# A diffusion step on one core: the last step of an adaLN quarter moves from VectorE to products in the bank, with a written order for two stages

## The chip, the cores and the metric

The kernel runs on one core of a Trainium2 chip. The metric is the device time of one execution in microseconds. An execution of the kernel before was also recorded by the hardware profiler; the rows quoted below come from that record. Engine names: PE is TensorE's matmuls, PEld its weight loads, DVE is VectorE, ACT is ScalarE, POOL is GpSimd, SP is SyncE, which issues nearly all DMA transfers.

## The reference, cut to what matters

One step of a two-layer network with d = 2048 over two groups of 128 tokens: a context pass and a denoising step. Both use the same weights. Every layer does this, once per group:

```python
mod = silu(cond) @ w_ada[l] + b_ada[l]              # 2048 -> 6 * 2048
sh1, sc1, gt1, sh2, sc2, gt2 = split(mod, 6)
h = rmsnorm(x, g_norm_mix[l]) * (1 + sc1) + sh1
m = mixer(h)                                        # layer 0: A + B, layer 1: C
x = x + gt1 * m
h = rmsnorm(x, g_norm_ffn[l]) * (1 + sc2) + sh2
x = x + gt2 * conv_ffn(h)                           # 2048 -> 2 * 5632 -> conv -> 2048
```

Mixer A + B (latent attention and grouped attention) has one input projection `w_in_ab` and one output projection `w_out_ab`; mixer C (differential attention) has `w_in_c` and `w_out_c`. A final RMSNorm and the six new cache tensors end it. All is float32. `cond` has one row per group, so `mod` has two columns for each of its 12288 elements, while its weights `w_ada` are 2 x 2048 x 12288 floats.

## The kernel before, in words

**Layout.** Activations lie transposed: features on the 128 partitions in 16 chunks, and 256 columns, the first 128 tokens of one group and the next 128 of the other. Every weight tile of 128 x 128 is split into a rounded high part `wh` (a copy by ScalarE, L244) and a low part `wl` (a subtraction by VectorE, L245); activations are split likewise. A tile costs three products of 256 columns (`gemm`, L104 through a helper, so all plain products have line 104; transposes have line 107). SyncE loads weights in tiles `raw` of up to 1 MB, from three buffers.

**Units.** A *unit* is a quarter (4 chunks, 512 elements) of one of the adaLN vectors of one layer, and streams 4 MB of `w_ada`. There are three ways to compute one.

- A unit of the list `ROWS` normally goes over TensorE. `row_step` loads four tiles `araw` (or `raw`) and `sum_rows` adds each into the one PSUM bank `ada`: the condition vector is the stationary side (128 x 32, two columns used), and the partial sums of four partition groups land in rows 32g and 32g+1 of the bank.
- A *side* unit (those listed in `BESIDE`, 3 in the first layer and 6 in the second) is summed by VectorE: `side_step` loads one `block` of 256 KB and `sum_block` adds it, scaled, into `aacc` (L481, two instructions a block, 16 blocks a unit). `reduce` then sums over partitions with four groups of products into the bank `misc`.
- Others go by a VectorE reduction over rows (`feature_step`, L452). They do not change.

The first two ways end in `ada_finish`, as a list of calls that are made one at each pump: `copy` (ScalarE copies the bank to `am` in SBUF, L408), then `turn`. The old `turn` transposes `am` in four blocks of 128 (two for a side unit) into a bank; VectorE then adds the partial sums with a reduce (L424; wide units) and adds the bias from the constants (L426, or L420 for a side unit) into `mod`, and for a scale vector forms the product with the norm's weights (`scales`). In the very first quarter, `half_unit` does half a unit at a time, in the same way; it is not changed.

**Stages.** The projection `w_in_ab` is done in parts over the input chunks, since the adaLN quarters come one after the other: two halves of the first quarter (h0 and h1), then quarters 1, 2, 3. Each `part` runs 23 output chunks; after a chunk it adds the result to the running sum (or copies it, the first time) and calls `pump`. Before a part `modulate` turns the normed x into the split `hx` for that quarter (VectorE `nt`, L596 and L602, ScalarE `hx`, L606), and `ensure` first finishes the two units (shift and scale) which that needs. After that come the heads of the first mixer, `w_out_ab`, norm, ConvFFN, then layer 1 in the same way.

**What sets the order.** The framework's scheduler orders the instructions of each engine by data and by its estimates, except where `keep_order` pins an instruction behind the pinned one before it. With `pe.in_turn` every TensorE instruction is pinned; before the change that is so in mixer C alone. `pump` spreads the units over the stages: it calls `side_pump` and `row_step` by rates per chunk (`RATE`, `SIDE`). `side_pump` adds the stage's `SIDE` rate to a due count and does one `side_step` per whole number; `side["apart"]` makes reduce, copy and turn wait one chunk each. `pinned[0]` pins the sums of rows from quarter 3 on, and puts each tile's sums some steps behind its load. `ada` has one buffer, `misc` one, `am` one, `block` three, and `raw` three.

## Time and profile before

| | us |
|---|---|
| median of 3 runs | 2364.11 (2363.92 to 2364.25) |
| the profiled execution | 2362.85 |
| its span | 2361.1 |
| PE busy | 2306.7 |
| DVE busy | 1847.8 |
| ACT busy | 1164.5 |
| POOL busy | 175.7 |

The span is the time from the first to the last record of the profiled execution; 1.75 us of its time lie around it. Busy times count matmuls, weight loads, vector and scalar operations, not the instructions that only issue transfers. In a timeline row the first number is the start in us from the span's start, the second the length, then engine, line, operation, output, inputs, and sizes; a bracket at the end gives how long the engine had been idle before it and what released it. In a row of groups, a count with x is followed by durations in ns.

The stages by start, in us: first part of `w_in_ab` 27.8 to 53.7, second half to 85.5, quarter 1 to 130.4, quarter 2 to 174.7, quarter 3 to 214.2, heads to about 331, output projection to 455.2, norm and first ConvFFN to 1188, layer 1 with mixer C to 1540, its output projection to 1613.6, the norm and second ConvFFN to about 2347.

### The profile page before, as it was taken

The page shows a single profiled execution, that of the slowest core. Times are in us where ns is not written, and L with a number is a line of the kernel's source. Part 1 is how long each engine was busy: PE and PEld are TensorE (multiplying, and loading weights), DVE is VectorE, ACT ScalarE, POOL GpSimd, SP SyncE. Part 2 cuts the span into 40 slices and gives each one's busy share as a digit, 9 for nine tenths or more (in the row PEclk, how much of TensorE's full clock was granted, in tenths as well). Part 3 has the DMA queues.
Part 4 walks back from the last instruction along what each step waited for, and adds up shares of the span by engine and source line. Part 5 has one row for each costly group of instructions (what it writes and reads, how often), then busy time and mean ns, then how long its engine had stood idle before and what let it go on. Part 6 is the DMA issues. An engine that isn't in the chain of part 4 may idle for free. (4 is left out here: it accounts for less than half of the span.)

```text
span 2361.1 us, 47623 instructions
## 1 busy us (share of the span) xinstructions
PE 2306.7 (98%) x19624; PEld 2183.2 (92%) x19624; DVE 1847.8 (78%) x2822; ACT 1164.5 (49%) x1857; POOL 175.7 (7%) x210
## 2 busy tenths in 40 slices
PE   6999999999999999999999999999999999999997
PEld 4778768899999999999989999998999999999997
DVE  3569866779999999999878888798899755666654
ACT  4245544465553355554464444446555534555543
POOL 0002202100000000001220000022000000000011
PEclk9999999999999999999999999999999999999999
DMA  9988888667777877777768888777677555555553
GB/s 368 360 310 283 310 316 328 248 241 251 261 265 285 303 268 260 262 259 274 285 249 279 306 295 312 249 242 271 245 260 258 198 194 197 197 195 191 192 193 124
DMA packets 108249, 612.96 MB, mean 260 GB/s; under 512 B 11712, under 2 KB 19584, under 8 KB 40832
## 3 DMA queue, kind: packets, MB, share of 16 engines
q1 hardware_dynamic: 108032, 609.92, 71.3%
q8 instruction: 154, 2.52, 0.4%
q14 instruction: 63, 0.52, 0.1%
HBM read 605.12 MB, written 4.75 MB: 258 GB/s over the span
## 5 line engine op out<-in xcount | busy, mean ns | idle before, releaser
L104 PE MATMUL acc<-hx,wh 128*128 128x256 f32 x8416 | 1456.3, 278 | 9.3 <-ACT hx L606 4.4
L104 PEld LDWEIGHTS acc<-hx,wh 128*128 128x128 f32 x8416 | 1272.6, 188 | 46.8 <-issue 16.6
L244 ACT CAST wh<-raw 128x1024 fp32r<-128x1024 f32 (+1 forms) x822 | 795.3, 978 | 943.1 <-PE acc L104 759.7
L245 DVE TENSOR_TENSOR wl<-raw,wh 128x1024 fp32r<-128x1024 f32 (+1 forms) x822 | 923.8, 1141 | 315.6 <-ACT wh L244 310.4
L104 PE MATMUL acc<-hx,wl 128*128 128x256 f32 x4208 | 1167.6, 278 | 2.5 <-DVE wl L245 2.3
L104 PEld LDWEIGHTS acc<-hx,wl 128*128 128x128 f32 x4208 | 790.7, 188 | 20.1 <-issue 7.1
L104 PE MATMUL acc<-g,wh 128*128 128x256 f32 x2816 | 478.8, 276 | 0.0
L104 PEld LDWEIGHTS acc<-g,wh 128*128 128x128 f32 x2816 | 423.4, 188 | 0.0
L104 PE MATMUL acc<-g,wl 128*128 128x256 f32 x1408 | 388.0, 276 | 0.0
L452 DVE CUSTOM_DVE_ANT_0 junk<-araw,condb 128x2048 f32<-128x2048 f32 x120 | 274.7, 2289 | 0.0
L104 PEld LDWEIGHTS acc<-g,wl 128*128 128x128 f32 x1408 | 264.2, 188 | 0.0
L481 DVE SCALAR_TENSOR_TENSOR aacc<-block,condw,aacc 128x512 f32<-128x512 f32 x270 | 199.0, 769 | 9.3 <-DMA block<-w_ada 9.0
L200 POOL TENSOR_TENSOR sqacc<-sqacc,sq 128x256 f32<-128x256 f32 x62 | 91.3, 1472 | 1507.6 <-issue 1210.6
L1127 ACT ACTIVATE cv<-acc,convw 128x256 f32<-128x256 f32 x176 | 98.2, 558 | 5.1 <-PE acc L104 5.1
L104 PE MATMUL acc<-oall,wh 128*128 128x256 f32 x512 | 90.3, 281 | 1.8 <-DVE oall L245 1.1
L104 PE MATMUL ada<-araw,condw 128*32 128x512 f32 (+1 forms) x608 | 77.4, 591 | 13.6 <-DMA araw<-w_ada 13.0
L656 DVE SCALAR_TENSOR_TENSOR x<-acc,mod,x 128x128 f32<-128x128 f32 x192 | 58.1, 343 | 39.6 <-PE acc L104 39.6
L1130 DVE SCALAR_TENSOR_TENSOR cv<-acc,convw,cv 128x254 f32<-128x254 f32 x176 | 83.6, 475 | 6.1 <-ACT cv L1127 6.1
L1133 DVE SCALAR_TENSOR_TENSOR cv<-acc,convw,cv 128x254 f32<-128x254 f32 x176 | 84.4, 479 | 3.6
L104 PEld LDWEIGHTS acc<-oall,wh 128*128 128x128 f32 x512 | 78.4, 191 | 2.7 <-DVE oall L245 1.3
L104 PE MATMUL acc<-oall,wl 128*128 128x256 f32 x256 | 71.4, 280 | 0.0
L196 ACT ACTIVATE sq<-x 128x256 f32<-128x256 f32 x75 | 31.0, 415 | 36.2 <-DVE x L656 32.4
(194 smaller groups left out, 1273.7 us busy)
## 6 DMA issues: line engine op xcount, KB each, us to landing
raw<-w_up SPq DMA_DIRECT2D x176, 1024.0 KB, 4.8
araw<-w_ada SPq DMA_DIRECT2D x142, 1024.0 KB, 5.8
raw<-w_down SPq DMA_DIRECT2D x88, 1024.0 KB, 4.8
raw<-w_in_c SPq DMA_DIRECT2D x48, 1024.0 KB, 6.6
block<-w_ada SPq DMA_DIRECT2D x144, 256.0 KB, 5.2
raw<-w_in_ab SPq DMA_DIRECT2D x19, 1024.0 KB, 6.1
raw<-w_out_ab SPq DMA_DIRECT2D x16, 1024.0 KB, 7.4
raw<-w_out_c SPq DMA_DIRECT2D x16, 1024.0 KB, 6.9
```

Of the source, the lines that this page charges most:

```text
L104: return self.placed(nc.tensor.matmul(*a, **kw))
L196: act.activation(sq, src, AF.Square)
L200: eng.tensor_tensor(out=st["acc"], in0=st["acc"], in1=sq, op=ALU.add)
L244: pin(act.copy(out_hi, src))
L245: pin(dve.tensor_tensor(out=out_lo, in0=src, in1=out_hi.bitcast(F32), op=ALU.subtract))
L452: keep_order(dve.tensor_tensor_reduce(out=T_(feat["pool"], [P, D], "junk"), in1=feat["row"][:, c], in0=feat["raw"].rearrange("p g n -> p ( ...
L481: i = dve.scalar_tensor_tensor(out=acc[c], in0=block, scalar=condw[:, k, c:c + 1], in1=acc[c], op0=ALU.mult, op1=ALU.add)
L656: dve.scalar_tensor_tensor(out=x[:, c, s], in0=ps[:, s], scalar=mod[:, l, 3 * which + 2, c, g:g + 1], in1=x[:, c, s], op0=ALU.mult, op1=AL ...
L1127: pin(act.activation(y, ps, AF.Identity, scale=cw[:, 1, m:m + 1], bias=cw[:, 3, m:m + 1]))
L1130: pin(dve.scalar_tensor_tensor(out=y3[:, :, 1:], in0=p3[:, :, :T - 1], scalar=cw[:, 0, m:m + 1], in1=y3[:, :, 1:], op0=ALU.mult, op1=ALU.add))
L1133: pin(dve.scalar_tensor_tensor(out=y3[:, :, :T - 1], in0=p3[:, :, 1:], scalar=cw[:, 2, m:m + 1], in1=y3[:, :, :T - 1], op0=ALU.mult, op1=A ...
```

## The change

The last step of a unit. `turn` opens the bank with a product of the identity and the bias (8 columns), then accumulates one product for each block of 128 columns of `am`: `am`'s block is the stationary side, and the moving side is a small constant that picks and adds the partial sums (`sel`, 2 columns, for a wide unit; 4 columns of the identity for a side unit). ScalarE copies the 8 finished columns from the bank to `mod`. The transposes, the reduce and the adds on VectorE go. A side unit's `am` gets a buffer of its own, `amside`. The constant `sel` takes two columns from `mhalf`.

The order. In the first part, `W.ahead` loads and splits the first weights, pinned, before `modulate`; in the second half the weights object is made ahead of `modulate` too. Quarters 1 and 2 run with `pe.in_turn`, so TensorE does its instructions as they are written; the units and the modulate of quarter q+1 are written at chunk 18 of quarter q, with the rows of `rows(q + 1)`.

Side units. Their loads are issued by `side_load`, two blocks ahead of the sums, and `side_start` issues the first two in pinned order on SyncE's queue. The rates `SIDE` are others.

In the order of instructions this gives: in the first part three `block` loads no longer stand early on SyncE's queue but follow at the start of quarter 3; two copies to `am` precede the first `wh` splits on ScalarE; half a unit's sums precede the first product of the projection. In the second half the `wl` splits precede `modulate` on VectorE. In quarters 1 and 2 the turn of a unit stands 12 products behind its last sums, where it stood right behind them. The third side unit of the first layer turns within the output projection `w_out_ab`, where it turned at the norm behind it. At the end of mixer C the last split of the attention output precedes three side sums on VectorE, and the last side unit of layer 1 turns in the shadow of the norm ahead of the second ConvFFN.

```diff
-    ("ident", 128), ("ones", 128), ("pick", 32), ("inv", 5), ("mhalf", 16),
+    ("ident", 128), ("ones", 128), ("pick", 32), ("inv", 5), ("mhalf", 14), ("sel", 2),
...
-SIDE = {"in3": 0.6, "heads": 1.05, "out0": 0.9, "c": 1.7, "outc": 2.0}
+SIDE = {"in3": 0.7, "heads": 1.0, "out0": 1.3, "c": 1.8, "outc": 2.0}
...
         def copy():
             n = NT if on_dve else 512
-            am = T_(tmp, [P, 512], "am", bufs=1)
+            if acc is None:
+                am = T_(tmp, [P, 512], "am", bufs=1)
+            else:
+                am = T_(side["pool"], [P, NT], "amside", bufs=1)
...
-            for b in range(2 if on_dve else 4):
-                pin(pe.transpose(pt[:, b * P:(b + 1) * P], got["am"][:, b * P:(b + 1) * P], ident))
             out = mod[:, l, j, 4 * q:4 * q + 4]
             bias = vector("bada", l, j, q)
+            to = pt[:, :8]
             if on_dve:
                 two = lambda v: v.rearrange("p (h b) c -> p b c h", b=2)
-                dve.tensor_tensor(
-                    out=two(out), in1=two(bias), op=ALU.add,
-                    in0=pt[:, :NT].rearrange("p (b c h r) -> p b c h r", b=2, c=2, h=2)[:, :, :, :, 0])
+                out_, bias = two(out), two(bias)
+                to = to.rearrange("p (b c h) -> p b c h", b=2, c=2)
+                pick = ident.rearrange("p (g n) -> p g n", g=4)[:, :, 0]
             else:
-                dve.tensor_reduce(out=out, in_=pt.rearrange("p (b g r) -> p b r g", b=4, g=4)[:, :, 0:2],
-                                  axis=AX.X, op=ALU.add)
-                dve.tensor_tensor(out=out, in0=out, in1=bias, op=ALU.add)
+                out_ = out
+                to = to.rearrange("p (b c) -> p b c", c=2)
+                pick = C("sel")
+            pin(pe.matmul(to, ident, bias, start=True, stop=False, skip_group_check=True))
+            n = 2 if on_dve else 4
+            for b in range(n):
+                pin(pe.matmul(pt[:, 8 // n * b:8 // n * (b + 1)], got["am"][:, b * P:(b + 1) * P], pick,
+                              start=False, stop=(b == n - 1), skip_group_check=True))
+            act.copy(out_, to)
...
+    def side_load(pin=lambda i: i):
+        n, k = divmod(side["at"], KD)
+        if n < len(side["all"]):
+            u = side["all"][n]
+            block = T_(side["pool"], [P, 512], "block", bufs=3)
+            pin(sp.dma_start(out=block, in_=A["w_ada"][u[0], u[1], u[2], k // 4][:, k % 4]))
+            side["ahead"].append(block)
+            side["at"] += 1
...
-        block = T_(side["pool"], [P, 512], "block", bufs=3)
-        sp.dma_start(out=block, in_=A["w_ada"][u[0], u[1], u[2], k // 4][:, k % 4])
-        sum_block(side["acc"], block, k)
+        side_load()
+        sum_block(side["acc"], side["ahead"].pop(0), k)
...
+        side.update(units=[ROWS[u] for u in units], all=[ROWS[u] for u in units], at=0, pool=pool_,
+                    rate=SIDE[name], due=0.0, apart=apart)
+        for _ in range(2):
+            side_load(keep_order)
...
-                def part(W, k0, n, first, rate, between=None, **kw):
+                def part(W, k0, n, first, rate, between=None, then=None, **kw):
...
+                        if c == 18 and then:
+                            then()
                         pump(rate, **kw)
...
                 for h in range(2):
+                    W = Weights(A["w_in_ab"][3 * h:3 * h + 3], 2, 8, cycle=23)
+                    if h == 0:
+                        W.ahead(keep_order)
                     modulate(hx, rb0, 0, 0, range(2 * h, 2 * h + 2))
-                    W = Weights(A["w_in_ab"][3 * h:3 * h + 3], 2, 8, cycle=23)
...
-                for q in range(1, 4):
+
+                def rows(q):
                     ensure(0, 1, [q])
                     ensure(0, 0, [q])
-                    pinned[0] = q == 3
-                    if q == 3:
+                    modulate(hx, rb0, 0, 0, range(4 * q, 4 * q + 4))
+
+                rows(1)
+                for q in range(1, 4):
+                    pe.in_turn = q < 3
+                    if q < 3:
+                        part(W, 4 * q, 4, False, RATE["in"], then=lambda: rows(q + 1), until=2 * (q + 2))
+                    else:
+                        pinned[0] = True
                         caches()
                         side_start("in3", BESIDE[0], beside)
-                    modulate(hx, rb0, 0, 0, range(4 * q, 4 * q + 4))
-                    if q < 3:
-                        part(W, 4 * q, 4, False, RATE["in"], until=2 * (q + 2))
-                    else:
                         part(W, 4 * q, 4, False, RATE["in3"], finish)
```

6 lines of the change are left out of this document (3 added, 3 removed).

## The prediction

> **What bounds the kernel now.** I read the page's share of the span by engine first, then the span in slices, then windows of single stages.
>
> ```profile
> span 2361.1 us, 47623 instructions
> PE 2306.7 (98%) x19624; PEld 2183.2 (92%) x19624; DVE 1847.8 (78%) x2822; ACT 1164.5 (49%) x1857; POOL 175.7 (7%) x210
> PE   6999999999999999999999999999999999999997
> 27.80:53.70 25.90, 24.51 (x207) 20.34 (x207) 9.38 (x17) 15.13 (x36) 0.73 (x1) 0.88 0.96 383
> 53.70:85.50 31.80, 29.24 (x219) 20.30 (x219) 18.61 (x44) 10.35 (x18) 2.43 (x3) 0.95 0.93 372
> 85.50:130.40 44.90, 42.24 (x350) 34.47 (x349) 27.82 (x53) 14.48 (x22) 2.14 (x2) 1.00 0.86 327
> 130.40:174.70 44.30, 44.17 (x342) 35.01 (x341) 24.22 (x47) 15.92 (x23) 2.52 (x2) 1.00 0.83 313
> 174.70:214.20 39.50, 38.68 (x324) 35.99 (x323) 39.38 (x77) 25.09 (x54) 9.81 (x10) 1.00 0.77 263
> 500.00:1188.00 688.00, 688.00 (x6073) 688.00 (x6072) 629.13 (x790) 342.55 (x450) 24.63 (x14) 1.00 0.73 267
> ```
>
> In the window rows the columns are the stretch, its length, busy time (instructions) of PE, PEld, DVE, ACT and POOL, the granted TensorE clock, the DMA share and GB/s. TensorE is busy for 98% of the span and without a gap through the first ConvFFN, where it does a product of 256 columns every 688.00/6073 = 113 ns. So every product added costs its full time, unless it falls into a gap, and a gain must come from a gap or from a stretch at half clock. Gaps lie before 175 us: the first four stretches of w_in_ab (two halves, two quarters) lack 1.39 + 2.56 + 2.66 + 0.13 = 6.7 us. Three windows, in the same columns, show half clock:
>
> ```profile
> 27.40:34.20 6.80, 6.39 (x38) 4.68 (x42) 1.26 (x3) 1.49 (x5) 0.73 (x1) 0.50 1.01 420
> 78.60:82.00 3.40, 3.40 (x16) 2.58 (x20) 3.05 (x7) 2.70 (x5) 1.69 (x2) 0.50 0.97 354
> 1539.50:1542.90 3.40, 3.40 (x19) 3.40 (x18) 3.22 (x7) 3.27 (x5) 0.05 (x1) 0.50 0.37 92
> ```
>
> Each follows a pause of TensorE, and half clock through 3.4 us loses 1.7 us. The Trainium skill, "TensorE: Matmul & The Clock Gate", section "What's actually happening", describes a gate that halves the clock after an idle window of about 3.4 us that runs freely; the lengths here (3.4, 3.4 and twice 3.4 us) agree. By that a shorter pause need not keep the clock full, so I count each later window as half won.
>
> **The last step of a unit.** A unit is a quarter of one adaLN vector; 22 come from TensorE's sums, 9 from VectorE's (side units), as the counts of the old adds below show (L426 x22, L420 x9). The old turn is four transposes (two for a side unit), then a reduce and an add on VectorE. The new one is a bias product and four (two) products accumulated in the bank, then a copy by ScalarE.
>
> ```profile
> L107 PE MATMUL ada<-cst,am x84: 270/273/421, 19.5 to 1502.2; 128*128 128x128 f32 x84
> L424 DVE TENSOR_REDUCE mod<-ada 128x8 f32<-128x32 f32 x19 | 3.6, 187 | 12.6 <-PE ada L107 12.6
> L426 DVE TENSOR_TENSOR mod<-mod,cst 128x8 f32<-128x8 f32 x22 | 3.6, 162 | 0.3
> L420 DVE TENSOR_TENSOR mod<-misc,cst 128x8 f32<-128x8 f32 x9 | 1.5, 166 | 2.4 <-PE misc L107 2.4
> 149.66 0.28 PE L104 MATMUL acc<-hx,wl 128*128 128x256 f32 x1
> 149.77 0.60 PE L107 MATMUL ada<-cst,am 128*128 128x128 f32 x4
> 150.44 0.28 PE L104 MATMUL acc<-hx,wl 128*128 128x256 f32 x1
> 228.69 0.34 PE L104 MATMUL acc<-kv_in,wh 128*128 128x384 f32 x1
> 228.87 0.50 PE L104 MATMUL misc<-cst,sq 128*128 128x1 f32 x4
> 229.49 0.34 PE L104 MATMUL acc<-kv_in,wl 128*128 128x384 f32 x1
> ```
>
> The first row counts 84 transposes: 19 units by four, and 8 in half units, which do not change. In the timeline rows (start, us, engine, line, operation) starts tell more than durations. From product to product over four transposes pass 150.44 - 149.66 = 0.78 us; the two products behind which they stand take 0.11 each and one more such product follows within the record, 0.34 in all, so four transposes insert 0.44 us. A plain f32 product with a narrow right side has two records: the four records from 228.87 are two products, and with two products of 384 columns (1.5 x 113 ns, 0.17 each) they span 0.80, so they insert 0.45, or 0.226 each. That is the nearest row: same stationary size, one column where the new turn has two, four or eight.
>
> New turn: 5 x 0.226 = 1.13 against 0.445 us, +0.685, by 22 units +15.1. Side unit: 3 x 0.226 = 0.68 against 0.23, +0.45, by 9 units +4.1. Together **+19.2 us** on TensorE, where nothing hides it except in gaps. VectorE loses 22 x (187 + 162) ns and 9 x 166, some 9 us, nearly all beside TensorE; ScalarE gains 31 copies, busy at 49%. From below, one record each at 0.113 would make the turn 0.57, and the sum +3.6; from above, exposed latency adds up to the 0.3 us of an engine handover (the 0.28 below) per unit, +8. I take 0.226, since the `sq` row is the same form.
>
> The Trainium skill, same page, section "Wait — 56ns, not 53.3ns?", says that start to start never drops below about 25 ns however narrow the product. By that floor alone ten records would be an estimated 0.25 us and the turn cheaper than the transposes, and the change would win; the `sq` row stands at 113 ns for a record, as if its weight load set it.
>
> The unit bank is single. Where the written order puts the next unit's sums right behind a turn, TensorE now waits for ScalarE's copy as it did for VectorE's reduce; two such places in the new order at about 0.5 us: **+1.0**. In mixer C two reductions of a side unit's sums by products now stand as two pairs in place of one group of four; at some 0.75 each, an estimate between the 0.44 of a split sum (below) and twice that: **+1.5**.
>
> **The head (h0).** The first weight pieces are now split ahead of modulate, the first `am` copies go ahead of these splits on ScalarE, and three side loads (0.75 MB of w_ada) leave the head of SyncE's queue for the third quarter's start.
>
> ```profile
> block<-w_ada SPq DMA_DIRECT2D x144, 256.0 KB, 5.2
> 24.72 0.36 ACT L369 COPY am<-ada 128x256 f32<-128x256 f32 x1
> 27.81 1.01 PE L104 MATMUL acc<-hx,wh 128*128 128x256 f32 x3 [2.23 <-ACT hx L606]
> 53.67 0.50 PE L104 MATMUL acc<-hx,wh 128*128 128x256 f32 x2 [1.16 <-ACT hx L606]
> ```
>
> Removing 0.75 MB at the window's 383 to 420 GB/s brings what is queued behind them up to 1.9 us forward, but the first product waits for `hx` off ScalarE, not for a load: I give it 0.8. A half unit's eight products at half clock (1.9 us) now run in that wait instead of behind it: 1.9. The gap of 1.16 at 53.67 loses 0.8, as the weights there no longer compete with modulate. Sum 3.5. The loads come back in the third quarter, where the DMA share of 0.77 leaves SyncE's queue room; a side load takes 5.2 us from issue to landing and is asked for two sums ahead. That costs nothing unless weights queued behind them run late, and then 1.9 us.
>
> **The second half (h1).**
>
> ```profile
> 76.14 1.12 DVE L602 TENSOR_SCALAR nt<-nt,scl,mod 128x128 f32<-128x128 f32 x4
> 77.17 2.09 DVE L245 TENSOR_TENSOR wl<-raw,wh 128x1024 fp32r<-128x1024 f32 x2
> 78.44 0.48 PE L104 MATMUL acc<-hx,wl 128*128 128x256 f32 x1 [1.51 <-DVE wl L245]
> ```
>
> The `wl` split stands behind modulate's `nt` on VectorE and TensorE waits 1.51. In the new order it stands ahead: 1.4 won, and half of the clock window behind it, 0.85. Head and halves: **-5.75**.
>
> **Quarters 1 and 2, in written order.**
>
> ```profile
> 100.78 0.66 PE L107 MATMUL ada<-cst,am 128*128 128x128 f32 x4 [0.71 <-ACT am L408]
> 101.72 1.07 PE L104 MATMUL ada<-araw,condw 128*32 128x512 f32 x8 [0.28 <-DVE mod L424]
> 126.69 0.39 PE L104 MATMUL acc<-hx,wl 128*128 128x256 f32 x1 [0.63 <-DVE wl L245]
> 141.07 1.05 PE L104 MATMUL ada<-raw,condw 128*32 128x512 f32 x2
> ```
>
> Turns now stand 12 products (1.4 us) behind their last sums, which covers the copy to `am`: twice 0.71 + 0.28, and smaller ones, 2.3. Sums kept in fours in place of five split ones (x2 as at 141.07, about 0.44 each): 2.2. With modulate at chunk 18 of the running part, the `wl` waits (0.63 and smaller ones) go: 1.4. Together **-5.9**. A written order also waits for what is late. Each quarter streams 44.3 us x 313 GB/s, 13.9 MB, which at the head's 383 to 420 GB/s take 33 to 36 us, so loads can lead; I take **+0.8**, about one late tile a quarter at the waits seen (0.3 to 0.7).
>
> **The first layer's end, and the heads.**
>
> ```profile
> 344.95 0.33 PE L107 MATMUL att<-cst,p 128*128 128x128 f32 x1 [0.86 <-DVE p L713]
> 455.34 0.38 PE L107 MATMUL misc<-cst,am 128*128 128x128 f32 x2
> 458.73 0.38 PE L104 MATMUL att<-cst,sq 128*128 128x1 f32 x2 [2.90 <-ACT sq L196]
> 1190.67 0.38 PE L104 MATMUL att<-cst,sq 128*128 128x1 f32 x2 [1.65 <-ACT sq L196]
> ```
>
> At other rates the third side unit turns long before the norm, no longer in it at 455.34. The same norm elsewhere waits 1.65 for 2.90; with the turn and what follows it I take **-2.0**. The wait of 0.86 at 344.95 can hide one turn: **-0.9**.
>
> **Mixer C and its end.**
>
> ```profile
> 1535.69 2.07 DVE L481 SCALAR_TENSOR_TENSOR aacc<-block,condw,aacc 128x512 f32<-128x512 f32 x3
> 1537.67 0.69 DVE L245 TENSOR_TENSOR oall<-att,oall 128x512 fp32r<-128x512 f32 x1
> 1538.42 0.39 PE L104 MATMUL acc<-oall,wh 128*128 128x256 f32 x1 [1.12 <-DVE oall L245]
> ```
>
> Three side sums stand ahead of the last split of `oall`; in the new order it comes first. 1.05 of the wait goes and half of the clock window, 0.85: **-1.9**. The last side unit's turn now lies in the final norm's shadow: **-0.9**.
>
> **Sum.** Costs 19.2 + 1.0 + 1.5 + 0.8 = 22.5; gains 5.75 + 5.9 + 2.0 + 0.9 + 1.9 + 0.9 = 17.35; net **+5.2 us**. The profiled execution took 2362.85, its span 2361.1 with 1.75 around it, 1.26 below the median of 2364.11. 2362.85 + 5.2 is 2368.05 for such an execution, and 2364.11 + 5.2 = **2369.3** for the median.
>
> **The rivals.**
>
> *Every gap goes (faster).* If the first product starts 2 us earlier, all three half-clock windows close (3.2 + 1.7 + 1.7 = 6.6 in place of the 1.7 counted) and w_in_ab loses all of its 6.7 us, gains are 17.35 + 4.9 + 2 + 2 = 26, and the time 2360. For it: each window follows a pause that the new order shortens. Against: the head's pause is set by ScalarE's chain to `hx`, which stays. It decides if the second half begins by about 49 us in place of 53.7.
>
> *Gains and costs cancel (same).* One window closes in full and a turn costs 0.15 less, because its first product overlaps: 5.2 - 0.85 - 22 x 0.15 = +1, time 2365.
>
> *The written order stalls (slower still).* If late loads or copies hold the quarters so that only half of their 5.9 and of the head's 5.75 come: +5.8, time 2375.
>
> *A narrow product at its floor (faster by far).* At 25 ns for a record, the turn would insert 0.25 instead of 0.445; 19.2 becomes -5, the time 2345. The `sq` row speaks against it: 113 ns in the same form.
>
> **How the numbers follow.** About 0.2% (4.7 us) is what a measurement of this kernel can tell from no change. My forecast, 2369.3, has 0.40 with 2366 to 2372 as its own range, and lies just on the slower side of that bound (2368.8): 0.24 slower, 0.16 same. Cancelling has 0.17, all of it same. The stall has 0.20, slower. Every gap gone has 0.20 and the floor 0.03, faster. That gives 0.23 faster, 0.33 same, 0.44 slower. The range runs from 2354, which takes in the third case with a turn at 0.9 us (22 x 0.23 = 5 lower), to 2377, the stall with 2 us of late weights.
>
> **What would show it.** Right: small products in a turn insert about 1.1 us, PE's busy time grows by some 15 us or more, no `nt` ahead of `wl` near 77 us, no half clock near 1540, the wait at the first layer's norm near 1.7. Wrong: a turn of under 0.8 us, or the first part's granted clock at 1.00 in place of 0.88, which would move it below 2362; or PE waits on `araw` or `mod` in the quarters above 2 us, which would move it above 2372.

## The result: 14 us slower, and where they are

The changed kernel took 2377.80 us (median of 6 runs, 2373.54 to 2381.02), the kernel before, on the same chip, 2364.02 (6 runs, 2361.62 to 2365.25). The ratio is 1.0059 with a 95% interval of 1.0046 to 1.0072, so 11 to 17 us more. Forecast were 2369.3 and a range up to 2377.0: the sign was right, the size was not, and the time lies 0.8 us outside the range. In two later sets 5 of 65 executions of the kernel before, and one each of e5 and e11, took 2391.0 to 2393.2 us, 26 to 29 longer than the median of their kernel, about what one ConvFFN loses in e8 and e14 below; none of them was profiled, so why stays open.

The page of the changed kernel begins so:

```profile
span 2375.4 us, 47941 instructions
PE 2325.4 (98%) x19792; PEld 2205.6 (93%) x19792; DVE 1843.4 (78%) x2771; ACT 1171.5 (49%) x1890; POOL 165.9 (7%) x210
```

TensorE has 168 more records of products (6 in each of 22 units, 4 in each of 9) and 18.7 us more busy time; VectorE has lost 51 instructions and 4 us. The timeline of TensorE in the changed kernel shows what one turn costs (start, us, engine, line, operation):

```profile
144.90 0.28 PE L104 MATMUL acc<-hx,wl 128*128 128x256 f32 x1
145.02 0.28 PE L104 MATMUL ada<-cst 128*128 128x8 f32 x2
145.16 1.03 PE L104 MATMUL ada<-cst,am 128*128 128x2 f32 x8
146.05 0.48 PE L104 MATMUL acc<-hx,wh 128*128 128x256 f32 x2
146.37 0.28 PE L104 MATMUL acc<-hx,wl 128*128 128x256 f32 x1
```

From 144.90 to 146.37 pass 1.47 us; three products of 256 columns take 0.34 of them, so the ten records insert 1.13 us, as forecast to the hundredth. The turns between products of 256 columns in the other stages show the same 1.13 to 1.14.

The starts of TensorE's accumulated products have the same order in both kernels, so stage times can be read from product to product. The first five columns are the parts of `w_in_ab` (two halves, quarters 1 to 3), then the heads, the first layer's end up to its norm, the stretch from the second layer's end over its norm, and everything in one number. Each row is one profiled execution; the other kernels are those of the experiments below.

| us | h0 | h1 | q1 | q2 | q3 | heads | layer 0's end | layer 1's norm | span |
|---|---|---|---|---|---|---|---|---|---|
| before | 25.9 | 31.8 | 44.9 | 44.3 | 39.5 | 145.2 | 105.6 | 55.5 | 2361.1 |
| changed | 25.5 | 29.9 | 45.7 | 44.0 | 42.2 | 154.3 | 105.3 | 55.1 | 2375.4 |
| changed, old turn (e1) | 25.6 | 29.6 | 48.0 | 44.2 | 42.0 | 149.7 | 102.7 | 55.4 | 2364.7 |
| before, new turn (e2) | 26.5 | 31.0 | 48.8 | 45.1 | 40.3 | 148.4 | 106.6 | 64.1 | 2381.8 |
| changed, old rates (e3) | 25.1 | 29.8 | 50.6 | 44.4 | 41.3 | 150.3 | 103.2 | 64.2 | 2380.2 |
| before, head alone (e5) | 26.3 | 28.7 | 47.8 | 44.5 | 39.5 | 145.4 | 105.3 | 56.7 | 2362.9 |
| before, quarters alone (e6) | 25.1 | 30.3 | 46.0 | 43.3 | 39.2 | 145.7 | 106.4 | 56.7 | 2362.4 |
| before, side units alone (e7) | 23.1 | 32.9 | 43.0 | 43.6 | 42.0 | 146.3 | 102.5 | 54.8 | 2358.9 |
| before, side units and turn (e13) | 22.8 | 32.7 | 47.4 | 41.7 | 42.0 | 151.6 | 106.3 | 55.6 | 2376.0 |

Both ConvFFNs take about the same in all of these (720.8 to 725.0 us each). In the changed kernel the first four parts won 1.8 us in sum and the first product came 0.9 us earlier, 2.8 in all, where the forecast gave -10.85 for their steps and +4.1 for six turns, -6.75; quarter 3 lost 2.7, and the heads 9.1, of which eight turns explain 5.0. The windows show quarters 1 and 2, quarter 3, and the place in the heads where it is worst (columns as in the prediction):

```profile
82.30:128.00 45.70, 44.83 (x361) 36.26 (x362) 26.78 (x48) 15.84 (x24) 1.46 (x2) 1.00 0.87 316
128.00:171.90 43.90, 43.76 (x361) 35.75 (x361) 23.42 (x43) 16.15 (x25) 1.63 (x2) 1.00 0.92 347
171.90:214.10 42.20, 39.54 (x324) 36.34 (x323) 41.53 (x79) 25.90 (x55) 9.83 (x10) 1.00 0.75 258
350.80:358.00 7.20, 5.71 (x23) 3.43 (x24) 3.00 (x11) 2.05 (x6) 0.41 (x2) 0.53 0.64 251
```

In quarter 3 VectorE is busy for 41.53 of 42.20 us: it is VectorE's stage, not TensorE's (39.54). It was so before (39.38 of 39.50, a row that the prediction quotes and didn't use). In the heads the timeline of the changed kernel has this:

```profile
341.89 0.33 SPq L553 DMA_DIRECT2D araw<-w_ada  x1
343.93 0.33 SPq L498 DMA_DIRECT2D block<-w_ada  x1
344.49 0.33 SPq L553 DMA_DIRECT2D araw<-w_ada  x1
...
350.10 1.42 DVE L489 SCALAR_TENSOR_TENSOR aacc<-block,condw,aacc 128x512 f32<-128x512 f32 x2 [2.94 <-DMA block<-w_ada]
351.43 0.42 DVE L245 TENSOR_TENSOR hx<-att,hx 128x256 fp32r<-128x256 f32 x1
351.76 0.15 DVE L731 RECIPROCAL rec<-sums 128x2 f32<-128x2 f32 x1
351.95 0.29 DVE L732 TENSOR_SCALAR p<-p,rec 128x128 f32<-128x128 f32 x1
352.29 0.48 PE L107 MATMUL att<-cst,p 128*128 128x128 f32 x1 [3.95 <-DVE p L732]
```

A side sum stands in VectorE's queue ahead of the softmax's last step and waits 2.94 us for its block, which was issued at 343.93, between two unit tiles of 1 MB; TensorE waits 3.95 us for `p`, and from 351.2 the clock is at half for 6.8 us. VectorE's waits for blocks, first in the changed kernel, then in the kernel before (us in total, times, longest):

```profile
DVE aacc L489 <- DMA block<-w_ada: 20.5, 10, 3.7
```

```profile
DVE aacc L481 <- DMA block<-w_ada: 9.0, 8, 2.5
```

Loads two blocks ahead were meant to shorten these waits. In this execution they doubled. In e1, e4, e7 and e13, whose side units are the same, the line reads 8.4, 9.6, 10.2 and 6.5 us, about what it was before, and none of the four has a wait for `p` there. So the loads ahead alone do not make the place at 350 us; of the other kernels e14 has it again (4.1 us).

### The profile page after: what moved, and what is told of

It is laid out like the page before. It is cut to its first block, busy times and chain, and to the rows that moved or that the text cites. A ratio compares the mean times of both kernels' runs of the same rounds, so it can differ in the third digit from the quotient of the medians.

```text
span 2375.4 us, 47941 instructions
## 1 busy us (share of the span) xinstructions
PE 2325.4 (98%) x19792; PEld 2205.6 (93%) x19792; DVE 1843.4 (78%) x2771; ACT 1171.5 (49%) x1890; POOL 165.9 (7%) x210
## 4 chain that ended last, share of the span: by engine, by line
PE 89%; DVE 5%; DMA 3%; issue 2%; ACT 1%; POOL 0%; DVEq 0%; SPq 0%; ACTq 0%; POOLq 0%
PE acc L104 82%; PE ada L104 4%; PE att L104 2%; DMA raw<-w_in_ab 2%; DVE wl L245 1%; PE misc L104 1%; DMA block<-w_ada 1%; DVE aacc L489 1%; PE att L107 1%; ACT wh L244 1%; DVE nt L615 0%; DVE nt L621 0%; DMA x<-xT 0%; DVE sqacc L200 0%; DVE x L1247 0%
## 5 line engine op out<-in xcount | busy, mean ns | idle before, releaser
L104 PEld LDWEIGHTS acc<-hx,wh 128*128 128x128 f32 x8416 | 1274.7, 188 | 47.8 <-issue 20.8
L244 ACT CAST wh<-raw 128x1024 fp32r<-128x1024 f32 (+2 forms) x824 | 795.5, 976 | 968.2 <-PE acc L104 779.4
L245 DVE TENSOR_TENSOR wl<-raw,wh 128x1024 fp32r<-128x1024 f32 (+2 forms) x824 | 920.8, 1134 | 317.1 <-ACT wh L244 311.9
L489 DVE SCALAR_TENSOR_TENSOR aacc<-block,condw,aacc 128x512 f32<-128x512 f32 x270 | 199.6, 772 | 20.7 <-DMA block<-w_ada 20.5
L104 PEld LDWEIGHTS acc<-oall,wl 128*128 128x128 f32 x256 | 48.0, 188 | 0.4 <-issue 0.4
```

Of the source, the lines that this page charges most:

```text
L104: return self.placed(nc.tensor.matmul(*a, **kw))
L244: pin(act.copy(out_hi, src))
L245: pin(dve.tensor_tensor(out=out_lo, in0=src, in1=out_hi.bitcast(F32), op=ALU.subtract))
L489: i = dve.scalar_tensor_tensor(out=acc[c], in0=block, scalar=condw[:, k, c:c + 1], in1=acc[c], op0=ALU.mult, op1=ALU.add)
```

## The experiments

Medians of the kernel before lie between 2363.67 and 2364.51 in the sets that follow; each ratio is to the kernel before in the same set.

**e1: the changed kernel with the old turn.**

```diff
-            pin(pe.matmul(to, ident, bias, start=True, stop=False, skip_group_check=True))
...
-            act.copy(out_, to)
+            for b in range(2 if on_dve else 4):
+                pin(pe.transpose(pt[:, b * P:(b + 1) * P], got["am"][:, b * P:(b + 1) * P], ident))
...
+                dve.tensor_reduce(out=out, in_=pt.rearrange("p (b g r) -> p b r g", b=4, g=4)[:, :, 0:2],
+                                  axis=AX.X, op=ALU.add)
+                dve.tensor_tensor(out=out, in0=out, in1=bias, op=ALU.add)
```

> The changed kernel with the old last step of a unit (transposes, then reduce and add on VectorE), all else as changed. Theory (the new turn costs 0.68 us a wide and 0.45 us a side unit on TensorE, 19.1 us in all, and nothing hides it): 2377.8 - 19.1 = 2358.7, with 168 fewer PE matmul records, and the wait of about 4 us near 350 us still there, since it is laid to side sums ahead of p on VectorE. Rival 1 (VectorE, given its reduces back in stages where it is full, returns part of it): 2364 or above. Rival 2 (the turn's copies on ScalarE also caused the wait near 350 us): 2353 or below.

Measured: 2361.07 us, ratio 0.9989 (0.9979 to 0.9998). The turn is worth 2377.80 - 2361.07 = 16.7 us, 2.4 below its price on TensorE; by the intervals of the two ratios this difference is uncertain by some 4 us, so it does not tell the theory from the first rival. One thing that the theory kept did not hold: the wait for `p` near 350 us is gone (TensorE's longest from 330 to 362 us is 1.6, for `mod`), though the side sums still stand on VectorE. All the rest of the change together is worth about 3 us of gain, where some 14 had been forecast.

**e2: the kernel before with the new turn alone.**

```diff
-                pin(pe.transpose(pt[:, b * P:(b + 1) * P], got["am"][:, b * P:(b + 1) * P], ident))
...
+            pin(pe.matmul(to, ident, bias, start=True, stop=False, skip_group_check=True))
...
+                pin(pe.matmul(pt[:, 8 // n * b:8 // n * (b + 1)], got["am"][:, b * P:(b + 1) * P], pick,
+                              start=False, stop=(b == n - 1), skip_group_check=True))
+            act.copy(out_, to)
```

> The kernel before with the new turn alone (and its constant). Theory: 2364.0 + 19.1 = 2383, every turn inserting 1.13 us in place of 0.445 us. Rival 1 (VectorE's relief of some 9 us shows in the third quarter and the heads, where it is nearly full): 2376 to 2380. Rival 2 (single bank and ScalarE's copy make it worse): above 2386.

Measured: 2382.12 us, 1.0069 (1.0053 to 1.0086): +17.7. The same from the other side, but in the profiled execution, 20.7 us longer than that of the kernel before, 8.6 of it fall on one place, the second layer's norm (64.1 us for 55.5). TensorE's waits there in this kernel:

```profile
PE att L104 <- POOL sqacc L200: 2.1, 1, 2.1
PE misc L104 <- DVE aacc L486: 1.4, 1, 1.4
PE att L104 <- ACT sq L196: 1.0, 1, 1.0
PE misc L104 <- ACT am L408: 0.5, 1, 0.5
PE misc L104 <- ACT mod L431: 0.3, 1, 0.3
```

With the old rates the last side unit ends in the norm: sums, copy and the new turn stand in line there, and the clock goes to half for 10.2 us from 1631.7 (so it does in e4 and e13 too, where this stretch takes 55.6, so the clock alone does not make the loss). The stretch just ahead of it is 3.4 us shorter (29.7 for 33.1), as the side unit's work has moved on, so the place costs 5.2 of the 20.7 us.

**e3: the changed kernel with the old rates.**

```diff
-SIDE = {"in3": 0.7, "heads": 1.0, "out0": 1.3, "c": 1.8, "outc": 2.0}
+SIDE = {"in3": 0.6, "heads": 1.05, "out0": 0.9, "c": 1.7, "outc": 2.0}
```

> The changed kernel with the rates of side sums as before (in3 0.6 for 0.7, heads 1.05 for 1.0, out0 0.9 for 1.3, c 1.7 for 1.8). Theory (the third quarter lost 2.7 us because VectorE was full there and got a sixth more side sums; the wait for p near 350 us and the half clock behind it, some 7 us together, come from where the third side unit starts): 2377.8 - 2.7 - 7 = 2368. Rival (the wait near 350 us comes from the loads issued ahead, whatever the rate): about 2375, with only the third quarter's loss gone. Second rival (rates do nothing): 2377.

Measured: 2380.63 us, 1.0067 (1.0052 to 1.0082). The theory missed by 12 us and the sign was wrong. Of its parts, quarter 3 gave back 0.9 of the 2.7 us (41.3 us at the old rate, for 39.5 in the kernel before, so the rate is not all of its loss) and the heads 4; but the second layer's norm took 64.2 for 55.1, as in e2, and quarter 1, in which nothing is different, took 50.6 for 45.7. So the changed rates belong to the new turn: they bring the last side unit out of the norm, where old rates and new turn together cost 9 us (e2, e3), less what the stretch ahead wins, and old rates with the old turn nothing (before: 55.5).

**e4: the changed kernel without the written order.**

```diff
-                    pe.in_turn = q < 3
```

> The changed kernel without the written order of TensorE in quarters 1 and 2 (modulate and turns still written at chunk 18; the scheduler places the products). Theory (the written order saves the waits behind sums and the split sums, some 4 us of the 5.9 forecast, and gives part back in waits): 2380, the loss inside 83 to 172 us. Rival (what was won there was won by writing modulate earlier; the written order itself waits for late tiles): 2375 to 2377.

Measured: 2375.39 us, 1.0046 (1.0031 to 1.0061), 2.4 below the changed kernel, which is no more than the scatter of single executions: the rival. The written order as such wins nothing that can be seen.

**e5: the kernel before with the order of head and halves alone.**

```diff
                 for h in range(2):
+                    W = Weights(A["w_in_ab"][3 * h:3 * h + 3], 2, 8, cycle=23)
+                    if h == 0:
+                        W.ahead(keep_order)
                     modulate(hx, rb0, 0, 0, range(2 * h, 2 * h + 2))
-                    W = Weights(A["w_in_ab"][3 * h:3 * h + 3], 2, 8, cycle=23)
```

> The kernel before with the change to the first part and the second half alone (weights object and first pinned weights ahead of modulate). The prediction gave this step -5.75, part of it by taking early side loads out of the queue, which this kernel does not do: some -3.9, 2360.5. Theory now (stalls read from one execution come back elsewhere, and stages scatter by some us from execution to execution, so single waits of about 1 us do not sum): -1 to -2, 2362.5 to 2363.5. Rival (the step is worth what was forecast): 2360.5.

Measured: 2363.86 us beside 2364.51, ratio 1.0002 (0.9974 to 1.0030). No gain that can be seen; the interval is wide and does not exclude the 3.9 of the expectation. h0 and h1 are 2.7 us shorter in its profile, and quarter 1 is 2.9 longer.

**e6: the kernel before with quarters 1 and 2 as changed.**

```diff
+                rows(1)
                 for q in range(1, 4):
+                    pe.in_turn = q < 3
...
-                        part(W, 4 * q, 4, False, RATE["in"], until=2 * (q + 2))
+                        part(W, 4 * q, 4, False, RATE["in"], then=lambda: rows(q + 1), until=2 * (q + 2))
```

> The kernel before with quarters 1 and 2 as changed (TensorE in written order, turns and modulate of the next quarter at chunk 18), old turn. The prediction gave -5.9 + 0.8 = -5.1, 2359.3. Theory now: 0 to -2, 2362.4 to 2364.4, with new waits for wl, wh or hx of some 2 to 4 us in 85 to 175 us in place of the turn's waits (2.2) and the split sums (2.2). Rival (the gain is there and lost elsewhere in the full change): 2359.3.

Measured: 2365.18 us, 1.0001 (0.9979 to 1.0022). TensorE's waits from 83 to 176 us, first of the kernel before, then of e6:

```profile
PE ada L107 <- ACT am L408: 1.5, 2, 0.8
PE acc L104 <- DVE wl L245: 0.8, 2, 0.6
PE ada L104 <- DVE mod L424: 0.6, 2, 0.3
```

```profile
PE acc L104 <- DVE wl L245: 3.2, 7, 0.9
PE acc L104 <- ACT wh L244: 0.2, 1, 0.2
```

The waits of the turn are gone, 2.1 us, and seven waits for `wl` have come, 3.2 us in place of 0.8. What releases them, in the timeline of e6:

```profile
116.98 2.00 ACT L244 CAST wh<-raw 128x1024 fp32r<-128x1024 f32 x2 [7.28 <-DMA raw<-w_in_ab]
118.06 2.36 DVE L245 TENSOR_TENSOR wl<-raw,wh 128x1024 fp32r<-128x1024 f32 x2 [0.74 <-ACT wh L244]
118.08 0.50 PE L104 MATMUL acc<-hx,wh 128*128 128x256 f32 x2 [0.23 <-ACT wh L244]
119.34 0.38 PE L104 MATMUL acc<-hx,wl 128*128 128x256 f32 x1 [0.76 <-DVE wl L245]
```

ScalarE had been idle for 7.28 us when the weight tile landed; then split, low split and product follow one another at once. TensorE has caught up with the loads here: what it saves at a turn it waits for at the next tile (e10 tests it).

**e7: the kernel before with the side units as changed** (loads two ahead, rates, own buffer), old turn, old order.

```diff
-SIDE = {"in3": 0.6, "heads": 1.05, "out0": 0.9, "c": 1.7, "outc": 2.0}
+SIDE = {"in3": 0.7, "heads": 1.0, "out0": 1.3, "c": 1.8, "outc": 2.0}
...
-        sp.dma_start(out=block, in_=A["w_ada"][u[0], u[1], u[2], k // 4][:, k % 4])
-        sum_block(side["acc"], block, k)
+        side_load()
+        sum_block(side["acc"], side["ahead"].pop(0), k)
...
+        for _ in range(2):
+            side_load(keep_order)
```

> The kernel before with the side units as changed: loads two blocks ahead, other rates, own buffer for their am; old turn. The prediction gave -2.0 (end of the first layer) - 0.9 - 1.9 - 0.9 + 1.5 = -4.2 and part of the head's gain (1.9 us of loads less ahead of the first products): 2359 to 2360. Theory now (the third quarter's VectorE is full, and more side sums there give back 2 to 3): 2362 to 2363. Rival (the waits it moves are worth nothing): 2364.4.

Measured: 2359.67 us, 0.9983 (0.9975 to 0.9992): -4.8 by the medians, where the prediction's steps gave -4.2, and up to 1.9 more for the moved loads, which it had counted with the head. The theory of this run (2362 to 2363) missed: quarter 3 did give back 2.5, and the total came out lower all the same. The sum was right; its parts are others. In windows of e7, the first part, and quarter 3 with the microsecond before it:

```profile
27.90:51.00 23.10, 22.28 (x195) 19.16 (x191) 9.29 (x17) 14.88 (x35) 0.74 (x1) 0.95 0.98 390
169.50:212.50 43.00, 40.39 (x334) 37.14 (x333) 42.08 (x82) 25.50 (x55) 11.40 (x10) 1.00 0.73 257
```

The first part is 2.8 us shorter without 0.75 MB in front of it, at a DMA share of 0.98 (22.8 to 23.3 us in e12, e13 and e15 too), and the second half 1.1 longer. Quarter 3 loses 2.5, with VectorE busy for 42.08 of 43.00.

**e8: the changed kernel with single-record products in the turn.**

```diff
-                am = T_(tmp, [P, 512], "am", bufs=1)
+                am = T_(tmp, [P, 512], "am", F32R, bufs=1)
...
-                pick = C("sel")
+                pick = pick2
...
+    picks = T_(keep, [P, 8], "picks", F32R)
+    pick4, pick2 = picks[:, 0:4], picks[:, 4:6]
+    act.copy(pick4, ident.rearrange("p (g n) -> p g n", g=4)[:, :, 0])
+    act.copy(pick2, C("sel"))
```

> The changed kernel with am and the picking constants in the rounded float32 form, so each picking product of a turn is one matmul record (this rounds am; the bias product stays in two records). Theory (a narrow product is priced by its records, 0.113 us each): a wide turn inserts 6 x 0.113 = 0.68 in place of 1.13, a side turn 4 x 0.113 = 0.45 in place of 0.68: 22 x 0.45 + 9 x 0.23 = 12 us less, 2366 beside 2377.8. Rival (the price is a product's, not a record's): 2378.

Measured: 2423.95 us, 1.0259. The turn did as the theory said:

```profile
146.96 0.28 PE L104 MATMUL acc<-hx,wl 128*128 128x256 f32 x1
147.07 0.28 PE L104 MATMUL ada<-cst 128*128 128x8 f32 x2
147.21 0.58 PE L104 MATMUL ada<-picks,am 128*128 128x2 f32 x4
147.66 0.48 PE L104 MATMUL acc<-hx,wh 128*128 128x256 f32 x2
147.98 0.28 PE L104 MATMUL acc<-hx,wl 128*128 128x256 f32 x1
```

From 146.96 to 147.98 pass 1.02 us, less 0.34 for three products: 0.68 for six records, 0.113 each. The price is a record's. From the first product to the 2500th this execution took 8.6 us less than the changed kernel's, where 16 turns and 3 side turns should give 16 x 0.45 + 3 x 0.23 = 7.9. But both ConvFFNs took 26 us longer each, which no theory had; e11 and e14 take that up.

**e9: the kernel before with less to load in the first parts.** The six units of these stages load a quarter of each tile and use it four times, so this kernel leaves out three quarters of those weights and its vectors are not the reference's.

```diff
-            sp.dma_start(out=ada["raw"], in_=A["w_ada"][l, j, q, t])
+            if ada["i"] < 8:
+                sp.dma_start(out=ada["raw"][:, 0], in_=A["w_ada"][l, j, q, t][:, 0])
+                ada["raw"] = ada["raw"][:, 0:1].to_broadcast([P, 4, 512])
+            else:
+                sp.dma_start(out=ada["raw"], in_=A["w_ada"][l, j, q, t])
```

> The kernel before, but the six units of w_in_ab's stages that go over TensorE (the third to the eighth of the list) load only the first quarter of each of their tiles and use it four times: 18 MB less to load before 175 us, same instructions (those vectors are left out in truth). Theory (from 28 to 175 us TensorE is paced by tiles that land 2.5 us a megabyte, or late for their split): the projection's 828th product starts at some 164 to 168 in place of 174.7, and the kernel takes 2355 to 2358. Rival (order on the engines sets these stages): 2363 to 2365.

Measured: 2353.35 us (2352.57 to 2354.15), 0.9950 (0.9930 to 0.9970): -10.3, and the 828th product at 166.0 us in place of 174.6. Windows of the kernel before, then of e9:

```profile
27.80:82.00 54.20, 50.25 (x396) 37.70 (x400) 25.20 (x54) 24.76 (x52) 3.16 (x4) 0.91 0.95 381
83.00:175.00 92.00, 89.20 (x714) 72.28 (x713) 54.15 (x102) 31.30 (x46) 4.67 (x4) 1.00 0.84 319
```

```profile
27.60:81.00 53.40, 51.98 (x424) 37.24 (x424) 28.53 (x58) 25.85 (x53) 3.10 (x4) 0.97 0.70 256
83.00:166.00 83.00, 83.00 (x672) 68.87 (x671) 52.56 (x94) 32.13 (x45) 2.98 (x4) 1.00 0.59 211
```

With the same work but 18 MB less to load, TensorE has no gap from 83 to 166 us and the clock stays near full. All of the gain before quarter 3 lies in quarters 1 and 2 (39.9 and 40.7 us for 44.9 and 44.3); the two halves together take 57.8 for 57.7. But the order is not the same: TensorE's order is the scheduler's here, and with smaller loads it sets the units' sums elsewhere, 32 of their records already in the first part, which takes 30.0 us for 25.9. So the 10.3 us are the worth of the smaller loads together with the order that they allow. What the loads of the kernel before wait for, from 83 to 175 us, is mostly TensorE itself, which frees a tile's buffer when it has done its sums:

```profile
SPq L291 <- PE ada L104: 40.9, 8, 7.8
```

The loads and the sums thus pace one another. The executions of e9 also scatter by only 1.6 us, but those of e10, with the same reduced loads, by 5.9 (2354.33 to 2360.22), so a small scatter does not come from the loads alone.

**e10: the same, with both changes of order.** e5's and e6's edits together with e9's:

```diff
+                    if h == 0:
+                        W.ahead(keep_order)
...
+                    pe.in_turn = q < 3
```

> The same reduced loads, with both changes of order (head and halves; quarters 1 and 2 in written order), old turn, old side units. Theory (the order's gain was eaten by loads that land late; with the loads out of the way the forecast 4 to 7 us show): 4 to 7 us below the run with reduced loads alone. Rival (the written order has waits of its own, loads or not): within 2 us of that run, or above it.

Measured: 2357.00 us, 0.9964 (0.9943 to 0.9984), 3.65 above e9. The rival: with the loads out of the way the written orders lose to the scheduler's. In quarters 1 and 2 TensorE has the same products in the same order here and in e6, so the two can be set side by side: e6's seven waits for `wl` (3.2 us) are gone, and the quarters took 86.5 us for 89.3, in one execution each. These waits came with the loads. TensorE's waits from 83 to 172 us have one line, and the timeline shows what is behind it:

```profile
PE ada L107 <- ACT am L408: 2.0, 2, 1.6
```

```profile
100.56 1.99 ACT L244 CAST wh<-raw 128x1024 fp32r<-128x1024 f32 x2 [7.36 <-DMA raw<-w_in_ab]
102.46 0.58 ACT L408 COPY am<-ada 128x512 f32<-128x512 f32 x1
103.09 0.33 PE L107 MATMUL ada<-cst,am 128*128 128x128 f32 x1 [1.64 <-ACT am L408]
```

The turn stands 12 products behind its sums, which I had taken to cover ScalarE's copy. But the copy stands behind two splits of weights, 1.99 us, and in a written order TensorE can't go on with the next products meanwhile.

**e11: 32 bytes more in SBUF.**

```diff
+    T_(keep, [P, 8], "shift")
     x = T_(keep, [P, KD, NT], "x")
```

> The kernel before with one unused tile of 8 floats a partition ahead of x, so all later SBUF addresses move by 32 bytes; no instruction changes. With the picking constants in a tile of that size, both ConvFFNs had taken 27 us longer each. Theory (addresses alone): 2364 + 54 = 2418, products of the ConvFFNs at 117.7 in place of 113.3 ns. Rival (the rounded form did it): 2364.

Measured: 2365.47 us, 1.0012 (0.9982 to 1.0043). The theory fell for this place of the tile, if the unused tile moved anything: the traces hold no addresses.

**e12: side units as changed, at a rate of 0.4 in quarter 3** (0.7) **and 1.1 in the heads** (1.0).

```diff
-SIDE = {"in3": 0.7, "heads": 1.0, "out0": 1.3, "c": 1.8, "outc": 2.0}
+SIDE = {"in3": 0.4, "heads": 1.1, "out0": 1.3, "c": 1.8, "outc": 2.0}
```

> The kernel before with the side units as changed (loads ahead), but at a rate of 0.4 in the third quarter (0.7 in the change) and 1.1 in the heads. Theory (VectorE is full in the third quarter, so each side sum less there saves about its time): the third quarter 39 to 40 us long in place of 42, the kernel 2357.5 beside 2359.7 with the changed rates. Rival (the quarter is longer because of the loads ahead, not the sums): 2360.

Measured: 2358.66 us, 0.9970 (0.9950 to 0.9990). Quarter 3 as a window of this kernel:

```profile
168.70:207.60 38.90, 38.20 (x324) 35.82 (x324) 36.98 (x77) 24.89 (x54) 12.21 (x11) 1.00 0.72 252
```

It takes 38.9 us in place of 42.0, and VectorE is no longer full (36.98 of 38.90): the theory, there. Of the 3.1 us only 1.0 reaches the median; in this execution the first layer's end took 106.3 us for e7's 102.5.

**e13: the kernel before with side units and turn as changed, in the old orders.** Against the changed kernel it is:

```diff
-                    if h == 0:
-                        W.ahead(keep_order)
...
-                    pe.in_turn = q < 3
...
-                        part(W, 4 * q, 4, False, RATE["in"], then=lambda: rows(q + 1), until=2 * (q + 2))
+                        part(W, 4 * q, 4, False, RATE["in"], until=2 * (q + 2))
```

> The kernel before with the side units and the new turn as changed, without both changes of order. Theory (the two changes of order are worth nothing measurable, with either turn): the changed kernel's time, 2376 to 2379. Rival (with the new turn the order is worth its 5 to 10 us, since there TensorE waits for ScalarE's copies right behind its sums): 2382 to 2388. Second rival (the order costs time, as it did with the loads out of the way): 2372 to 2375.

Measured: 2376.21 us, 1.0055 (1.0042 to 1.0069). The changed kernel, which differs by both orders only, took 2377.80 at 1.0059 (1.0046 to 1.0072). With the new turn too the orders are worth nothing that can be seen; the loss of 1.6 lies within the scatter.

**e14: the changed kernel with e8's picking tile in plain float32.**

```diff
-    picks = T_(keep, [P, 8], "picks", F32R)
+    picks = T_(keep, [P, 8], "picks")
```

> The changed kernel with the picking constants copied to a tile of their own in plain float32, at the place where the rounded ones lay; all products of a turn again in two records. Theory (the tile's place slowed the ConvFFNs by 27 us each): products of the ConvFFNs at 117.7 ns, 2431. Rival (the rounded form of am did it): 113.3 ns, 2378.

One execution: 2434.76 us. The same 100 us of the first ConvFFN, in the kernel before, in e14 and in e11:

```profile
600.00:700.00 100.00, 100.00 (x885) 100.00 (x884) 91.98 (x118) 53.27 (x74) 0.00 (x0) 1.00 0.72 262
```

```profile
600.00:700.00 100.00, 100.00 (x851) 100.00 (x850) 89.18 (x115) 50.71 (x71) 0.00 (x0) 1.00 0.69 253
```

```profile
600.00:700.00 100.00, 100.00 (x884) 100.00 (x884) 91.97 (x118) 53.21 (x74) 0.00 (x0) 1.00 0.72 260
```

A product takes 100/851 = 117.5 ns in place of 113.0, at full clock and without a gap. So it's the tile, not the form of the products. That it is the tile's place is argued, not shown: the same 32 bytes ahead of `x` (e11) do no harm, and what it is about this tile that matters stays open.

**e15: a version that beats both kernels.** Side units as changed, old turn, old orders, rates 0.4 in quarter 3, 1.15 in the heads, 1.6 in the first output projection.

```diff
-SIDE = {"in3": 0.7, "heads": 1.0, "out0": 1.3, "c": 1.8, "outc": 2.0}
+SIDE = {"in3": 0.4, "heads": 1.15, "out0": 1.6, "c": 1.8, "outc": 2.0}
```

> The kernel before with loads of side units ahead, rates 0.4 in the third quarter, 1.15 in the heads, 1.6 in the first output projection, so that the third unit turns as early as in the changed kernel (2017 products into the projections against 2184 with 1.1 and 1.3). Theory (the third quarter at 39 us and the first layer's end at 102.5 us can both be had): 2355 to 2357. Rival (what VectorE does not do in the third quarter it does in the heads, at the same price): 2359 to 2360.

Measured: 2357.61 us, 0.9976 (0.9967 to 0.9984), between theory and rival, and the lowest median of those that leave nothing out, though its lead over e12 and e7 lies within the scatter. By its interval it is some 4 to 8 us, 0.2%, below the kernel before. Quarter 3 took 38.9 us and the heads 143.1 for 145.2; the first layer's end took 106.2, so its 102.5 in e7 doesn't come from an early turn.

## Why the prediction was wrong

The sum was +19.2 (turn) + 1.0 (copies) - 4.2 (side units: -2.0, -0.9, -1.9, -0.9, +1.5) - 5.75 (head and halves) - 5.1 (quarters) = +5.2. Measured are 16.7 and 16.5 (turn: the changed kernel less e1, and e13 less e7), -4.8 (side units, e7), and +1.4 and +1.6 (both orders: e1 less e7, and the changed kernel less e13). 16.6 - 4.8 + 1.5 = 13.3, beside 13.8 in all. By the intervals of the ratios each of these differences is uncertain by 3 to 4.5 us, the side units' by 2. The gain of the orders is the term that fails beyond that: -10.85 forecast, of which up to 1.9 belongs to the moved loads that e7 has, and nothing measured.

- *The turn* was right in its price (1.13 us, forecast 1.13). Its effect came out lower than 19.2 in all three comparisons (16.7, 16.5 and e2's 17.7), each time by less than the scatter of that comparison; if some 2 us do come back, VectorE's reduces and the waits for them, now gone, may be the place, and no run shows it. The rule that I had set against the row, from the Trainium skill, "TensorE: Matmul & The Clock Gate", section "Wait — 56ns, not 53.3ns?" (start to start not below about 25 ns), is a floor that these products stay far above: e8 has 0.113 us for a record with 2 columns, and the turn is dearer than the transposes.
- *Copies* at 1.0 us can't be told apart.
- *Side units* (the 0.9 of a wait in the heads is counted here) were right in the sum, by luck, and not in the parts. I costed the moved loads at nothing unless weights ran late. They brought 2.8 us in the first part, 1.1 of which went again in the second half (forecast within 0.8 for the first product). Quarter 3 cost 2.5 that I had not counted, since I read it as TensorE's: its row said VectorE 39.38 of 39.50, and at a rate of 0.4 it took 38.9 us (e12). The first layer's end, -2.0 forecast, won 3.1 in e7 and nothing in e12, e13 and e15. In the heads the reverse of what I asked for can happen: not weights behind blocks, but a block among unit tiles on SyncE's queue, with `p` behind the sum that waits for it; the changed kernel and e14 show it, e1, e4, e7 and e13 do not.
- *Head and halves* (-5.75) and *quarters* (-5.1) are the steps that failed. The waits of TensorE that I had listed went, and the time didn't. In the quarters a wait that is taken away at a turn comes back at the next weight tile (e6: 2.1 us gone, 2.4 come), and that comes from the loads: with 18 MB less and the same order the new waits are gone (e10). Without that limit the written order has a wait of its own, for a copy behind weight splits (e10). I had asked whether loads could lead at the rate of the head, found 33 to 36 of 44 us, and taken the rest for slack; the queue can't use it, since a tile is asked for only when a buffer comes free (SyncE's waits for TensorE's sums, 40.9 us in e9's section), and lands 5.5 to 7.3 us later by the medians before 175 us. For the head and the halves no run shows the reason: e5 gained nothing that can be seen, its halves 2.7 us shorter and its quarter 1 2.9 longer, and smaller loads did not shorten them (e9).
- *Half-clock windows* counted as half won (1.7 in sum) came and went. The prediction had three of them; the kernel before has three more of 3.4 us, at 460.9, 1191.3 and 1618.0, and those move too: the changed kernel has the one near 1540 us no more and 3.4 us less at the start, still has 3.4 us near 75, and got 6.8 us near 351 and 3.4 more near 471. The Trainium skill, same page, section "What's actually happening", says that the window runs freely, so that the same work meets it at other phases; the runs agree (quarter 1, below, where nearly the same waits bring 6.8 us at half clock in e3 and none in e14).
- *The rivals.* "The written order stalls" (2375, chance 0.20) was nearest in time and right that the gains don't come; its reason, late loads or copies that hold the quarters, is what e6 and e10 show there. The signs did not tell: those for the forecast came (1.13 us for a turn, 18.7 us more busy time, `wl` ahead of `nt` near 77 us, no half clock near 1540), and the one for the stall, waits on `araw` or `mod` in the quarters, did not, since the waits were for `wl`. The range ended 0.8 us short, since I let the gains fall by half at most, and not to nothing.

## What to carry to other kernels

A wait that the profile lists is worth its length only if what the engine does next is ready: before a gain is summed, ask whether the stage is paced by something behind the wait, here the loads, and test it by loading less with the order held, since a scheduler answers smaller loads with another order. Where one engine is full in a stage (VectorE in quarter 3), that engine prices every edit there, whatever the page's totals say. A narrow f32 product costs TensorE two records of 0.113 us, twice what a transpose of 128 columns costs, so work is not free because it is small.

## What the hardware showed that I had not expected

- The same written order of TensorE gives stages that differ by up to 5 us from execution to execution: quarter 1 took 45.7 us in the changed kernel, 50.6 in e3 and 48.0 in e14, in which TensorE has the same instructions up to there. In e3 a stretch of 6.8 us at half clock from 120.9 lies in it, in the other two none, though e14 has nearly e3's waits there (1.6 us for `wh` and 1.4 for `wl`; 1.4 and 1.4 in e3). Whole executions of the changed kernel spread by 7.5 us (2373.54 to 2381.02). A stage read from one execution is no measure of a gain of 1 or 2 us.
- With one more tile of 32 bytes a partition in SBUF each product of both ConvFFNs took 4.5 ns longer, 52 to 54 us in all (e8, e14); an unused tile of that size at another place did nothing (e11). Why is open.
- A block's landing sets VectorE's wait through the queue that it shares: 256 KB, 5.2 us from issue in the median of the kernel before, but over 6 us between two unit tiles of 1 MB (issued 343.93, sum at 350.10).
